# FF1 of two token blocks by seven half-depth products per pair of feature tiles, in a one-core diffusion step

## The chip, the cores and the metric

One core of a Trainium2 chip runs the whole program. The metric is the device time of one execution in microseconds (us). The engines are PE (TensorE, matrix products), DVE (VectorE), ACT (ScalarE), POOL (GpSimd) and SP (SyncE, which issues the DMAs here). Each engine works through its own queue in the order in which the program puts it there; waits between engines go by semaphores.

## What is computed

The kernel is one inference step of a one-layer backbone over 1152 tokens of 1024 features: 1024 latent tokens (chunks 0 to 7 of 128) and 128 context tokens (chunk 8). A state-space mixer and a gated MLP are merged and projected; what concerns the change is the end of the layer:

```python
x = layer_norm(DN_ALPHA * x + gate1 * (merged @ w_out), ln1_g, ln1_b)
h = x * (1.0 + scale2) + shift2
f = jnp.square(jax.nn.relu(h @ w_ff1)) @ w_ff2      # w_ff1 1024 x 4096, w_ff2 4096 x 1024
x = layer_norm(DN_ALPHA * x + gate2 * f, ln2_g, ln2_b)
```

## The kernel before

**Tiling.** Tokens go in three blocks of 384 (`TB`, three chunks of 128 each); blocks 0 and 1 are latent tokens, block 2 holds chunks 6, 7 and the context chunk 8. Every product is made to float32 precision by three passes of the reduced fp32r type: each operand is split into a rounded high part and a remainder (`split`: ACT copies `hi`, another engine subtracts to get `lo`), and `mm3` issues high by high (L89), high by low (L90) and low by high (L91).

**Output projection.** For each block b and each half of the 1024 output features, `tm_half` runs 4 weight tiles over three chunks. `ev_o` evicts: gate (`ot`, DVE), residual with `xr` (DVE), and after the second half the layer norm (`ln_stats` on DVE: per chunk two statistics and a dozen operations on single columns; then a normalization on ACT), a write of the row to `NX` in DRAM, 8 PE transposes per chunk, scale and bias per 128 x 128 square (DVE and ACT in turn), and the split into the activation operands `h2` (ACT and POOL). The residual inputs `xr` come by DMA into four buffers.

**FF1.** Each of 32 feature tiles takes one 128 x 1024 weight tile (`take_fm`, double buffered: raw, high, low) and multiplies it with the three blocks, 24 matmuls of 384 columns each, 72 per tile. `ev_h_of` evicts: relu on ACT, square on DVE, write to `HID` in DRAM. The first two tiles do blocks 0 and 1 first, then block 2.

**FF2.** For each block, 32 steps (`load2`, `split2`): load a weight row tile `w2` and the hidden tile `hraw`, split both (ACT high, DVE low), then 18 matmuls of 512 columns into six banks. `residual` prepares chunk c's final residual: load `NX` into `xa`, multiply by `row_g`, add `row_b`, two DVE operations of 128 x 1024 per chunk, all queued near the start of FF2.

**Order.** The code is written in one order, but the framework sorts each engine's queue by a schedule of its own when it builds the program, within buffers and dependencies. So the first FF2 weights and hidden tiles were loaded and split during FF1, and the weights of the first FF2 steps even during the output projection: their buffers were free.

Of the kernel before, what the change touches and what calls it, by code (L numbers as in the profile page):

```python
# [10 lines left out]
F32 = mybir.dt.float32  # L11
# [24 lines left out]
def tile_trunk(ctx: ExitStack, tc: tile.TileContext, I, O):  # L36
# [43 lines left out]
    def split(raw, hi, lo, eng):  # L80
        A.activation(hi, raw, AF.Copy)  # L81
        if eng is None:
            for e, cs in ((G, slice(0, 512)), (V, slice(512, D))):
                e.tensor_tensor(lo[:, cs], raw[:, cs], hi[:, cs], op=SUB)
        else:
            eng.tensor_tensor(lo, raw, hi, op=SUB)  # L86
# [8 lines left out]
    for n, src in (("xbc", [I["w_xbc"][i] for i in range(12)]),  # L95
                   ("gb", [I["w_gb"][i] for i in range(KT)]), ("ga", [I["w_ga"][i] for i in range(KT)]),
                   ("z", [I["w_z"][i] for i in range(KT)]),
                   ("v", [I["w_v"][i % 8] for i in range(24)]),
                   ("u", [I["w_u"][i] for i in range(KT)]),
                   ("pb", [I["w_proj_b"][i] for i in range(KT)]), ("pa", [I["w_proj_a"][i] for i in range(KT)]),  # L100
                   ("out", [I["w_out"][i % 8] for i in range(24)])):
        wsrc += [(n, s) for s in src]
    wsrc += [("ff1", I["w_ff1"][i]) for i in range(FT)]
    state = {"raw": 0, "split": 0, "use": 0}
    raws, pairs = deque(), deque()
    lo_eng = {"eng": lambda i: G}

    behind, FINE = {}, {0: 4, 1: 2}
# [736 lines left out]
    V.tensor_tensor(S2, modc[1][:, :, 0, :], l1[:, 0, :].unsqueeze(2).broadcast_to([P, KT, 2]), op=MUL)  # L845
    V.tensor_tensor(H2, modc[1][:, :, 0, :], l1[:, 1, :].unsqueeze(2).broadcast_to([P, KT, 2]), op=MUL)
    V.tensor_tensor(H2, H2, modc[1][:, :, 1, :], op=ADD)
    h2 = six("h2")
    for b in range(NB):
        xr = []  # L850

        def load_xr():
            loads = [dma(out=g1[b], in_=GROW[0, b].partition_broadcast(P))] if b < 2 else []
            for c in range(3 * b, 3 * b + 3):
                r = tO.tile([P, D], F32, name="xr", tag="xr", bufs=4)
                loads.append(dma(out=r, in_=XP[c] if c < NL else I["x_prompt"]))
                xr.append(r)
            for ins in loads:
                order(ins, state["last"])

        for half in range(2):
            def ev_o(tt, ps):
                c = 3 * b + tt
                v = 0 if c < NL else 1
                hs = slice(half * 512, (half + 1) * 512)
                t = tO.tile([P, 512], F32, name="ot", tag="ot", bufs=2)
                V.tensor_tensor(t, ps, g1[v][:, hs], op=MUL)
                V.scalar_tensor_tensor(xr[tt][:, hs], xr[tt][:, hs], ALPHA, t, op0=MUL, op1=ADD)
                if half == 0:
                    return  # L870
                r = xr[tt]
                mv = ln_stats([r[:, 0:512], r[:, 512:1024]], tO)
                A.activation(r, r, AF.Identity, bias=mv[:, 2:3], scale=mv[:, 1:2])
                dma(out=NX[c], in_=r)
                for hf in range(2):
                    tp = pxB.tile([P, 4, P], F32, name="h2_ps", tag="aux")
                    ht = tO.tile([P, 4, P], F32, name="h2t", tag="h2t", bufs=2)
                    for a in range(4):
                        k = hf * 4 + a
                        T.transpose(tp[:, a, :], r[:, k * P:(k + 1) * P], ident)  # L880
                    for a in range(4):
                        k = hf * 4 + a
                        if a % 2:
                            A.activation(ht[:, a, :], tp[:, a, :], AF.Identity, bias=H2[:, k, v:v + 1],
                                         scale=S2[:, k, v:v + 1])
                        else:
                            V.tensor_scalar(ht[:, a, :], tp[:, a, :], S2[:, k, v:v + 1], H2[:, k, v:v + 1],
                                            op0=MUL, op1=ADD)
                    split(ht, h2[b][0][:, hf * 4:hf * 4 + 4, tt * P:(tt + 1) * P],
                          h2[b][1][:, hf * 4:hf * 4 + 4, tt * P:(tt + 1) * P], G)  # L890

            tm_half(pmB, "out", mp[b], ev_o, load_xr if half == 0 else None)
# [5 lines left out]
    def ev_h_of(ft):
        def ev_h(b, ps):
            rl = tF.tile([P, 512], F32, name="rl", tag="rl", bufs=2)[:, 0:TB]  # L900
            A.activation(rl, ps, AF.Relu)  # L901
            V.tensor_tensor(rl, rl, rl, op=MUL)  # L902
            dma(out=HID[ft][:, b * TB:(b + 1) * TB], in_=rl)
        return ev_h
# [221 lines left out]
```

## Time and profile before

| | us |
|---|---|
| median of three runs | 1971.39 (1970.22 to 1972.48) |
| profiled execution | 1971.82 |
| its span, first to last instruction | 1970.0 |
| first matmul of FF1 | 1147.48 |
| first matmul of FF2 | 1567.08 |

Times inside the trace count from the start of the span. PE is busy 97% of it; the waits that there are can be read stage by stage. A group of instructions in the page stands as line, engine, operation, output and inputs with shapes, count, then busy time and the mean of one; matmuls overlap their successors, so the step from one start to the next is what one costs, not its duration.

### The profile page before, as it was taken

What the parts mean: (1) busy time and instruction counts of PE and PEld (TensorE: products, weight loads), DVE (VectorE), ACT (ScalarE), POOL (GpSimd) and SP (SyncE); (2) the same over time, 40 slices, a digit from 0 to 9 for tenths busy, and PEclk for the clock granted to TensorE, in tenths of its full rate; (3) what the DMA queues carried; (4) which work ended last, traced back from release to release, by engine and by line L of the source; (5) the groups of instructions that cost most, each with busy time, mean ns of one, the idle gap of its engine ahead of it and who ended that gap; (6) DMA issues with size and microseconds to landing.
All of it is one profiled execution on the core that took longest, in us unless ns stands there. A gap on an engine that the chain in (4) does not pass through costs nothing.

```text
span 1970.0 us, 28049 instructions
## 1 busy us (share of the span) xinstructions
PE 1911.4 (97%) x10747; PEld 1754.1 (89%) x10747; DVE 1110.6 (56%) x2031; ACT 684.2 (35%) x1186; POOL 341.3 (17%) x272
## 2 busy tenths in 40 slices
PE   7999999899999999999999979999999999999998
PEld 4999998788898889999998879999999988888886
DVE  4756857999798353444455873222222474754844
ACT  3443424555413332333332553211111233433431
POOL 0322002333224530254220120000000000000001
PEclk9999999999999999999999989999999999999999
DMA  8144635445575431188445654333223575565540
GB/s 342 58 133 165 209 140 163 129 151 153 194 241 158 121 106 42 33 289 285 140 139 179 203 214 119 107 107 92 91 88 91 184 263 177 168 218 177 182 163 32
DMA packets 139878, 307.58 MB, mean 156 GB/s; under 512 B 14880, under 2 KB 78048, under 8 KB 138592
## 3 DMA queue, kind: packets, MB, share of 16 engines
q1 hardware_dynamic: 139744, 305.80, 47.5%
q8 instruction: 84, 1.38, 0.3%
q14 instruction: 50, 0.41, 0.1%
HBM read 244.23 MB, written 61.51 MB: 155 GB/s over the span
## 4 chain that ended last, share of the span: by engine, by line
PE 82%; DVE 10%; issue 3%; DMA 3%; ACT 1%; POOL 1%; SPq 0%; POOLq 0%; DVEq 0%; ACTq 0%
PE mm_ps L89 19%; PE mm_ps L90 19%; PE mm_ps L91 19%; PE ff_ps L90 6%; PE ff_ps L91 6%; PE ff_ps L89 6%; DVE Fb L581 1%; PE y_ps L601 1%; DVE crow L241 1%; DVE X L662 1%; PE st_ps L523 1%; DVE cbD L584 1%; DVE ssq L670 1%; PE s_ps L734 1%; DVE ada_w L241 1%
## 5 line engine op out<-in xcount | busy, mean ns | idle before, releaser
L89 PE MATMUL mm_ps<-hTh,w_hi 128*128 128x384 f32 x1032 | 355.0, 348 | 0.6 <-ACT gt L620 0.6
L91 PE MATMUL mm_ps<-hTh,w_lo 128*128 128x384 f32 x1032 | 351.0, 340 | 0.0
L90 PE MATMUL mm_ps<-hTl,w_hi 128*128 128x384 f32 x1032 | 351.0, 340 | 0.0
L89 PE MATMUL mm_ps<-h,w_hi 128*128 128x384 f32 x768 | 258.6, 337 | 5.8 <-ACT h L81 5.8
L91 PE MATMUL mm_ps<-h,w_lo 128*128 128x384 f32 x768 | 257.6, 336 | 1.0 <-DVE w_lo L86 1.0
L90 PE MATMUL mm_ps<-h,w_hi 128*128 128x384 f32 x768 | 258.0, 336 | 0.4 <-POOL h L86 0.4
L81 ACT ACTIVATE w_hi<-w_raw 128x1024 fp32r<-128x1024 f32 (+1 forms) x143 | 147.5, 1033 | 277.0 <-PE mm_ps L90 170.3
L90 PE MATMUL ff_ps<-w,hid 128*128 128x512 f32 (+1 forms) x608 | 229.9, 378 | 0.0
L91 PE MATMUL ff_ps<-w,hid 128*128 128x512 f32 (+1 forms) x608 | 229.4, 378 | 0.0
L89 PE MATMUL ff_ps<-w,hid 128*128 128x512 f32 (+1 forms) x608 | 229.4, 378 | 0.0
L86 DVE TENSOR_TENSOR w_lo<-w_raw,w_hi 128x1024 fp32r<-128x1024 f32 (+2 forms) x109 | 135.5, 1245 | 160.9 <-ACT w_hi L81 160.6
L89 PEld LDWEIGHTS mm_ps<-hTh,w_hi 128*128 128x128 f32 x1032 | 195.0, 190 | 10.9 <-issue 7.9
L90 PEld LDWEIGHTS mm_ps<-hTl,w_hi 128*128 128x128 f32 x1032 | 195.1, 189 | 9.5 <-issue 7.0
L91 PEld LDWEIGHTS mm_ps<-hTh,w_lo 128*128 128x128 f32 x1032 | 194.9, 189 | 4.1 <-issue 4.1
L89 PEld LDWEIGHTS mm_ps<-h,w_hi 128*128 128x128 f32 x768 | 145.4, 190 | 6.5 <-ACT h L81 6.5
L902 DVE TENSOR_TENSOR rl<-rl 128x384 f32<-128x384 f32 x96 | 54.2, 565 | 170.4 <-ACT rl L901 170.4
L986 POOL TENSOR_TENSOR xa<-xa,row_lg 128x512 f32<-128x512 f32 (+1 forms) x11 | 15.5, 1421 | 764.9 <-ACT xa L985 638.9
L91 PEld LDWEIGHTS mm_ps<-h,w_lo 128*128 128x128 f32 x768 | 145.2, 189 | 1.3 <-DVE w_lo L86 1.3
L90 PEld LDWEIGHTS mm_ps<-h,w_hi 128*128 128x128 f32 x768 | 145.4, 189 | 0.9 <-POOL h L86 0.9
L86 DVE TENSOR_TENSOR w<-w,w 128x1024 fp32r<-128x1024 f32 x96 | 117.9, 1232 | 47.0 <-PE ff_ps L91 24.3
L89 PEld LDWEIGHTS ff_ps<-w,hid 128*128 128x128 f32 x608 | 114.4, 188 | 21.7
L90 PEld LDWEIGHTS ff_ps<-w,hid 128*128 128x128 f32 x608 | 114.4, 188 | 21.4
(251 smaller groups left out, 3351.9 us busy)
## 6 DMA issues: line engine op xcount, KB each, us to landing
w<-in_w_ff_dram SPq DMA_DIRECT2D x96, 512.0 KB, 5.0
HID<-rl SPq DMA_DIRECT2D x96, 192.0 KB, 2.1
hraw<-HID SPq DMA_DIRECT2D x96, 192.0 KB, 2.4
w_raw<-in_w_ff_dram SPq DMA_DIRECT2D x32, 512.0 KB, 4.0
w_raw<-in_w_v_dram SPq DMA_DIRECT2D x24, 512.0 KB, 3.7
w_raw<-in_w_out_dram SPq DMA_DIRECT2D x24, 512.0 KB, 3.7
Fb<-FB SPq DMA_DIRECT2D x36, 256.0 KB, 4.3
Bb<-FB SPq DMA_DIRECT2D x36, 256.0 KB, 5.0
```

Source lines behind the costliest of these rows:

```text
L81: A.activation(hi, raw, AF.Copy)
L86: eng.tensor_tensor(lo, raw, hi, op=SUB)
L89: T.matmul(ps, s[0], m[0], start=first, stop=False)
L90: T.matmul(ps, s[0], m[1], start=False, stop=False)
L91: return T.matmul(ps, s[1], m[0], start=False, stop=last)
L241: V.scalar_tensor_tensor(wt[:, i, :] if v else junk, wt[:, i, :], 1.0, crow[:, v, :], op0=MUL, op1=MUL, accum_out=outs[:, k, i, v:v + 1])
L523: ins = T.matmul(st, Bk[:, c, g * P:(g + 1) * P], xws[g].rearrange("p h e -> p (h e)"), start=True, stop=True)
L581: V.scalar_tensor_tensor(Fb[:, i, :], Bb[:, i, :], QT[:, c, 3, h:h + 1], Fb[:, i, :], op0=SUB, op1=MIN)
L584: V.scalar_tensor_tensor(cbD[:, i, :], cbL[:, g, :], QT[:, c, 0, h:h + 1], cbD[:, i, :], op0=MUL, op1=ADD)
L601: ins = T.matmul(yp[64 * i:64 * i + 64, q, :], lhs[:, l0 + 64 * j:l0 + 64 * j + 64], rhs[:, j, :], start=n == 0, stop=n == len(terms) - 1)
L662: V.scalar_tensor_tensor(y, xt.rearrange("p (c i) -> p c i", i=P), dskc[:, q:q + 1], y, op0=MUL, op1=ADD)
L902: V.tensor_tensor(rl, rl, rl, op=MUL)
```

## The change

FF1 of blocks 0 and 1 is made as a two by two block product (Strassen's scheme, with Winograd's sums): the two input halves of 512 features by the two token blocks by a pair of feature tiles. Seven products of half depth (12 matmuls each) take the place of eight (96 matmuls); block 2 is still multiplied directly (`direct`, 48 matmuls per pair). That makes 132 matmuls per pair and not 144.

- `combos` builds the activation operands: x11 and x21 after block 0 of the output projection, x22 and the sums q11, q12, q22, q21 with their splits xt4, xt2, xt3, xt1 after block 1. Each covers 128 x 1536.
- `sums` builds four sums of the pair's raw weights (128 x 512 each) and splits them; f0 and f1, the two weight tiles, are split as before.
- The results are combined at eviction: k1 copied by ACT, u2, u3 by DVE, `keep` adds the last term, relu and square in one DVE operation, and writes `HID`. A low half is on DVE everywhere in these stages; POOL has no part in it.
- In the output projection all scale and bias operations are on ACT; `xr` has three buffers and `ot` one; block 2's scale and bias are written in place over `xr`, whose write to `NX` must have landed first. In pair 0 the transposes of chunks 6 to 8 are put behind its half products, and `direct` of block 2 comes last.
- FF2's pool and its first loads come behind all of FF1 in the code.

```diff
+    def operand(name, src):
+        t = blk.tile([P, 2, 4, TB], F32R, name=f"x{name}", tag="blk", bufs=NBLK)
+        split(src, t[:, 0], t[:, 1], V)
+        X[name] = (t[:, 0], t[:, 1])
+
+    def combos(b):
+        q11, q21, q12, q22 = quad[0, 0], quad[1, 0], quad[0, 1], quad[1, 1]
+        if b == 0:
+            operand("11", q11)
+            operand("21", q21)
+            return
+        operand("22", q22)
+        V.tensor_tensor(q11, q12, q11, op=SUB)
+        V.tensor_tensor(q12, q22, q12, op=SUB)
+        V.tensor_tensor(q22, q22, q11, op=SUB)
+        V.tensor_tensor(q21, q22, q21, op=SUB)
+        for name, q in (("t4", q21), ("t2", q22), ("t3", q12), ("t1", q11)):
+            operand(name, q)
...
-                r = tO.tile([P, D], F32, name="xr", tag="xr", bufs=4)
+                r = tO.tile([P, D], F32, name="xr", tag="xr", bufs=3)
...
-                t = tO.tile([P, 512], F32, name="ot", tag="ot", bufs=2)
+                t = tO.tile([P, 512], F32, name="ot", tag="ot", bufs=1)
...
-                    ht = tO.tile([P, 4, P], F32, name="h2t", tag="h2t", bufs=2)
+                    ts = slice(tt * P, (tt + 1) * P)
+                    ht = r.rearrange("p (k f) -> p k f", f=P)[:, 4 * hf:4 * hf + 4, :] if b == 2 else quad[hf, b][:, :, ts]
                     for a in range(4):
                         k = hf * 4 + a
-                        T.transpose(tp[:, a, :], r[:, k * P:(k + 1) * P], ident)
+                        ins = T.transpose(tp[:, a, :], r[:, k * P:(k + 1) * P], ident)
+                        h_first.setdefault((c, hf), ins)
                     for a in range(4):
                         k = hf * 4 + a
-                        if a % 2:
-                            A.activation(ht[:, a, :], tp[:, a, :], AF.Identity, bias=H2[:, k, v:v + 1],
-                                         scale=S2[:, k, v:v + 1])
-                        else:
-                            V.tensor_scalar(ht[:, a, :], tp[:, a, :], S2[:, k, v:v + 1], H2[:, k, v:v + 1],
-                                            op0=MUL, op1=ADD)
-                    split(ht, h2[b][0][:, hf * 4:hf * 4 + 4, tt * P:(tt + 1) * P],
-                          h2[b][1][:, hf * 4:hf * 4 + 4, tt * P:(tt + 1) * P], G)
+                        A.activation(ht[:, a, :], tp[:, a, :], AF.Identity, bias=H2[:, k, v:v + 1],
+                                     scale=S2[:, k, v:v + 1])
+                    if b == 2:
+                        split(ht, h2b[0][:, hf * 4:hf * 4 + 4, ts], h2b[1][:, hf * 4:hf * 4 + 4, ts], V)
 
             tm_half(pmB, "out", mp[b], ev_o, load_xr if half == 0 else None)
+        if b < 2:
+            combos(b)
...
+    NP = FT // 2
+    S_HOME = [blk if p % 2 else blk2 for p in range(NP - 2)] + [blk, blk2]
+    low, high = slice(0, 512), slice(512, D)
+
+    def sums(p):
+        r0, r1 = raw_of.pop(FF0 + 2 * p), raw_of.pop(FF0 + 2 * p + 1)
+        pl = S_HOME[p]
+        t3 = pl.tile([P, 3, 2, 512], F32R, name="S", tag="blk", bufs=NBLK if pl is blk else NBLK2)
+        t4 = (tV if p % 2 else tW).tile([P, 2, 512], F32R, name="S4", tag="S4", bufs=1)
+        ops = [t3[:, 0], t3[:, 1], t3[:, 2], t4]
+        f = [tW.tile([P, 512], F32, name="sum", tag="sum", bufs=2) for i in range(2)]
+        for j, i, x, y, op in ((0, 2, r1[:, low], r1[:, high], ADD), (1, 1, r0[:, low], r1[:, low], SUB),
+                               (0, 0, f[0], r0[:, low], SUB), (0, 3, r0[:, high], f[0], SUB)):
+            V.tensor_tensor(f[j], x, y, op=op)
+            split(f[j], ops[i][:, 0, :], ops[i][:, 1, :], V)
+        return [(t[:, 0, :], t[:, 1, :]) for t in ops]
...
+    def half_product(s, x, cs=slice(0, 512)):
+        ps = pmB.tile([P, TB], F32, name="mm_ps", tag="mm")
+        for k in range(4):
+            ks = slice(cs.start + k * P, cs.start + (k + 1) * P)
+            done = mm3(ps, (s[0][:, ks], s[1][:, ks]), (X[x][0][:, k, :], X[x][1][:, k, :]), k == 0, k == 3)
+        return ps, done
...
+    def keep(p, ft, b, x, y=None, op=ADD):
+        t = (tV if p else tW).tile([P, TB], F32, name="sq", tag="sq", bufs=5 if p else 2)
+        if y is None:
+            A.activation(t, x, AF.Relu)
+            V.tensor_tensor(t, t, t, op=MUL)
+        else:
+            V.tensor_tensor(t, x, y, op=op)
+            V.scalar_tensor_tensor(t, t, 0.0, t, op0=MAX, op1=MUL)
+        dma(out=HID[ft][:, b * TB:(b + 1) * TB], in_=t)
...
+    def next_pair(p, f):
+        if p < NP:
+            nxt.append(take("ff1", 0, 1 - f))
+            if f == 1:
+                S.append(sums(p))
+                more_raw(state["use"] + 1)
+
+    nxt, S = [], deque()
+    next_pair(0, 0)
+    next_pair(0, 1)
+    for p in range(NP):
+        (f0, f1), nxt = nxt, []
+        s2, s3, s1, s4 = S.popleft()
+        ft = 2 * p
+        p1, e1 = half_product(f0, "11")
+        k1, u2, u3 = temp("k1"), temp("u2"), temp("u3")
+        A.activation(k1, p1, AF.Copy)
+        p2, e2 = half_product(f0, "21", high)
+        keep(p, ft, 0, p2, k1)
+        if p:
+            direct(p, ft, f0)
+            next_pair(p + 1, 0)
+        p4, e4 = half_product(f1, "t4", high)
+        if p:
+            direct(p, ft + 1, f1)
+            next_pair(p + 1, 1)
+        p6, e6 = half_product(s2, "t2")
+        V.tensor_tensor(u2, p6, k1, op=ADD)
+        p7, e7 = half_product(s3, "t3")
+        V.tensor_tensor(u3, p7, u2, op=ADD)
+        keep(p, ft + 1, 0, u3, p4, SUB)
+        p5, e5 = half_product(s1, "t1")
+        keep(p, ft + 1, 1, p5, u3)
+        V.tensor_tensor(u2, p5, u2, op=ADD)
+        p3, e3 = half_product(s4, "22")
+        keep(p, ft, 1, p3, u2)
+        if not p:
+            for c, after in ((6, (e4, e6)), (7, (e7, e5)), (8, (e3, e3))):
+                for hf in range(2):
+                    order(h_first[c, hf], after[hf])
+            direct(p, ft, f0)
+            next_pair(p + 1, 0)
+            direct(p, ft + 1, f1)
+            next_pair(p + 1, 1)
+    stV.close()
+    stW.close()
     tF = pool(stB, "tF")
...
-    w0, w1 = take_fm("ff1"), take_fm("ff1", 0)
-    for bs in ((0, 1), (2,)):
-        fm_tile(pmB, w0, h2, ev_h_of(0), bs)
-        fm_tile(pmB, w1, h2, ev_h_of(1), bs)
...
-    for ft in range(2, FT):
-        w = take_fm("ff1")
-        fm_tile(pmB, w, h2, ev_h_of(ft))
```

Three places show what becomes of the order. The first is DVE at the entry to FF1, from the last weight splits of the output projection (`w_lo` of out) on; before, it held residuals (`xr`, `ot`), scale and bias (`h2t`) and splits of FF2's first weights (`w2`):

```order
L868 SCALAR_TENSOR_TENSOR xr_10326<-xr_10326,ot_10530 128x512
L867 TENSOR_TENSOR ot_10579<-mm_ps_10432,g1_0_9580 128x512
L887 TENSOR_SCALAR h2t_10294<-h2_ps_10293,S2_9582,H2_9583 128x128
L887 TENSOR_SCALAR h2t_10306<-h2_ps_10305,S2_9582,H2_9583 128x128
L86 TENSOR_TENSOR w_lo_10682<-w_raw_10510,w_hi_10681 128x1024
```

```order
L86 TENSOR_TENSOR w_lo_10473<-w_raw_10452,w_hi_10472 128x1024
...
L868 TENSOR_TENSOR h2f0_9592<-h2f1_9593,h2f0_9592 128x1536
L940 TENSOR_TENSOR sum_10671<-w_raw_10500 128x512
L940 TENSOR_TENSOR sum_10672<-w_raw_10476,w_raw_10500 128x512
L86 TENSOR_TENSOR w_lo_10497<-w_raw_10476,w_hi_10496 128x1024
...
L869 TENSOR_TENSOR h2f1_9593<-h2f1_9593 128x1536
L86 TENSOR_TENSOR x22_10286<-h2f1_9593,x22_10286 128x1536
...
L870 TENSOR_TENSOR h2f1_9593<-h2f1_9593,h2f0_9592 128x1536
...
L871 TENSOR_TENSOR h2f0_9592<-h2f1_9593,h2f0_9592 128x1536
...
L86 TENSOR_TENSOR xt4_10293<-h2f0_9592,xt4_10293 128x1536
```

The sums of activations (L868 to L871) and the wide splits now stand between the weight splits, w_lo_10497 being that of the first feature tile and xt4 the operand of the third half product. The second place is ACT at the same entry, from the normalization of chunk 6 on (before L873, after L901):

```order
L873 ACTIVATE xr_10326<-xr_10326,ln_mv_10536 128x1024
...
L884 ACTIVATE h2t_10556<-h2_ps_10555,H2_9583,S2_9582 128x128
L884 ACTIVATE h2t_10568<-h2_ps_10567,H2_9583,S2_9582 128x128
...
L81 ACTIVATE h24_9593<-h2t_10556 128x4x128
L81 ACTIVATE h24_9593<-h2t_10568 128x4x128
```

```order
L81 ACTIVATE xt1_10302<-h2f0_9592 128x1536
L901 ACTIVATE xr_10316<-xr_10316,ln_mv_10526 128x1024
...
L913 ACTIVATE xr_10316<-h2_ps_10545,H2_9586,S2_9585 128x128 x4
L81 ACTIVATE h2h_10305<-xr_10316 128x4x128
L81 ACTIVATE S_10669<-sum_10671 128x512
L81 ACTIVATE S_10669<-sum_10672 128x512
L81 ACTIVATE S_10669<-sum_10671 128x512
L81 ACTIVATE S4_10670<-sum_10671 128x512
L81 ACTIVATE S_10869<-sum_10871 128x512
```

The high halves of pair 0's weight sums (S_10669, S4_10670) now stand behind the in-place scale and bias of chunk 6 (L913). The third place is DVE at the passage from FF1 to FF2; before, the splits of hidden tiles (`hid`) of the first nine FF2 steps stood among the evictions of FF1 (`rl`), and at the passage stood

```order
L963 TENSOR_TENSOR xa0_13676<-xa0_13676,row_g_13662 128x1024
L902 TENSOR_TENSOR rl_13645<-rl_13645 128x384
L963 TENSOR_TENSOR xa0_13676<-xa0_13676,row_g_13662 128x1024
L964 TENSOR_TENSOR xa0_13676<-xa0_13676,row_b_13664 128x1024
...
L86 TENSOR_TENSOR hid_13907<-hraw_13876,hid_13907 128x384
```

```order
L960 TENSOR_TENSOR sq_13853<-mm_ps_13840,u2_13699 128x384
L1064 TENSOR_TENSOR xa0_13889<-xa0_13889,row_g_13875 128x1024
L1065 TENSOR_TENSOR xa0_13889<-xa0_13889,row_b_13877 128x1024
L961 SCALAR_TENSOR_TENSOR sq_13853<-sq_13853 128x384
...
L86 TENSOR_TENSOR w2_14117<-w2_14087,w2_14117 128x1024
...
L1064 TENSOR_TENSOR xa2_13891<-xa2_13891,row_g_13875 128x1024 x3
L1065 TENSOR_TENSOR xa2_13891<-xa2_13891,row_b_13877 128x1024
L86 TENSOR_TENSOR hid_13872<-hraw_13864,hid_13872 128x384
```

sq_13853 is the last `keep` of FF1, which reads the last half product; hid_13872 is the first hidden tile of FF2. Between the two now stand 18 operations of 128 x 1024 (15 of `residual`, 3 splits of `w2`).

## Rows read from the trace of the kernel before

**Rows 1.** The page, part 1: busy time of each engine, share of the span, instructions
```profile
PE 1911.4 (97%) x10747; PEld 1754.1 (89%) x10747; DVE 1110.6 (56%) x2031; ACT 684.2 (35%) x1186; POOL 341.3 (17%) x272
```

**Rows 2.** The page, part 5: costliest groups, one pass of FF1's three; squares
```profile
L89 PE MATMUL mm_ps<-h,w_hi 128*128 128x384 f32 x768 | 258.6, 337 | 5.8 <-ACT h L81 5.8
...
L902 DVE TENSOR_TENSOR rl<-rl 128x384 f32<-128x384 f32 x96 | 54.2, 565 | 170.4 <-ACT rl L901 170.4
```

**Rows 3.** Timeline of PE, 1147 to 1569 us: start, duration, line, idle before
```profile
1147.48 0.42 PE L89 MATMUL mm_ps<-h,w_hi 128*128 128x384 f32 x1
...
1150.06 0.33 PE L90 MATMUL mm_ps<-h,w_hi 128*128 128x384 f32 x1
...
1151.97 0.33 PE L89 MATMUL mm_ps<-h,w_hi 128*128 128x384 f32 x1
...
1156.44 1.01 PE L89 MATMUL mm_ps<-h,w_hi 128*128 128x384 f32 x2 [3.27 <-ACT h L81]
1157.25 0.52 PE L90 MATMUL mm_ps<-h,w_hi 128*128 128x384 f32 x1
...
1161.41 0.52 PE L91 MATMUL mm_ps<-h,w_lo 128*128 128x384 f32 x1
...
1567.08 0.39 PE L89 MATMUL ff_ps<-w,hid 128*128 128x512 f32 x1
```

**Rows 4.** PE's waits from 1140 to 1200 us: total, times, longest
```profile
PE mm_ps L89 <- ACT h L81: 5.8, 2, 3.3
PE h_ps L880 <- ACT h2t L884: 3.7, 3, 3.1
```

**Rows 5.** Windows: length, busy time of each engine, granted clock, DMA share, GB/s
```profile
1080.00:1147.00 67.00, 67.00 (x317) 55.44 (x316) 57.30 (x153) 38.42 (x55) 13.78 (x10) 1.00 0.69 247
1147.00:1164.00 17.00, 12.74 (x60) 12.10 (x59) 17.00 (x29) 8.78 (x12) 3.74 (x3) 0.80 0.51 186
1164.00:1200.00 36.00, 29.44 (x160) 27.53 (x159) 15.60 (x56) 18.05 (x32) 7.48 (x6) 0.86 0.36 119
1200.00:1550.00 350.00, 350.00 (x2021) 350.00 (x2020) 82.58 (x119) 71.49 (x119) 0.00 (x0) 1.00 0.32 97
```

**Rows 6.** Lines of DVE, 1060 to 1200 us, by form: busy, mean ns
```profile
L867 DVE TENSOR_TENSOR ot<-mm_ps,g 128x512 f32<-128x512 f32 x17 | 11.4, 681 | 2.4 <-PE mm_ps L91 2.2
```

**Rows 7.** Lines of ACT, 1060 to 1200 us, by form
```profile
L884 ACT ACTIVATE h2t<-h_ps,H,S 128x128 f32<-128x128 f32 x36 | 15.6, 455 | 18.6 <-DVE h2t L887 18.6
L81 ACT ACTIVATE h<-h2t 128x512 fp32r<-128x512 f32 x18 | 10.9, 627 | 0.2
```

**Rows 8.** Timeline of DVE: a layer norm's small operations, then the passage
```profile
1120.81 0.14 DVE L197 TENSOR_SCALAR ln_mv<-ln_mv 128x1 f32<-128x1 f32 x1
...
1125.22 0.16 DVE L210 SCALAR_TENSOR_TENSOR ln_mv<-ln_mv 128x1 f32<-128x1 f32 x1
...
1569.37 1.22 DVE L963 TENSOR_TENSOR xa<-xa,row_g 128x1024 f32<-128x1024 f32 x1
...
1582.37 1.22 DVE L86 TENSOR_TENSOR w<-w,w 128x1024 fp32r<-128x1024 f32 x1
1583.50 1.22 DVE L963 TENSOR_TENSOR xa<-xa,row_g 128x1024 f32<-128x1024 f32 x1
...
1597.40 1.22 DVE L964 TENSOR_TENSOR xa<-xa,row_b 128x1024 f32<-128x1024 f32 x1
```

**Rows 9.** The page, part 6: DMA issues, KB each, us to landing
```profile
hraw<-HID SPq DMA_DIRECT2D x96, 192.0 KB, 2.4
w_raw<-in_w_ff_dram SPq DMA_DIRECT2D x32, 512.0 KB, 4.0
```

**Rows 10.** DMA issues from 1040 to 1200 us
```profile
NX<-xr SPq DMA_DIRECT2D x9, 512.0 KB, 4.5
...
xr<-XP SPq DMA_DIRECT2D x8, 512.0 KB, 6.0
```

**Rows 11.** DMA from 1140 to 1147 us, when the engines are full
```profile
DMA packets 769, 2.79 MB, mean 399 GB/s; under 512 B 91, under 2 KB 91, under 8 KB 768
```

More of the change, by code (lines that the diff above doesn't have):

```diff
@@ L102, in tile_trunk @@
         wsrc += [(n, s) for s in src]
+    FF0 = len(wsrc)
     wsrc += [("ff1", I["w_ff1"][i]) for i in range(FT)]
     state = {"raw": 0, "split": 0, "use": 0}
-    raws, pairs = deque(), deque()
+    raws, pairs, raw_of = deque(), deque(), {}
     lo_eng = {"eng": lambda i: G}
@@ L142, in more_split @@
             pairs.append((hi, lo))
+            raw_of[i] = raw
             state["split"] += 1
@@ L836, in tile_trunk @@
     lo_eng["eng"] = lambda i: V
+    stW = ExitStack()
+    tW = pool(stW, "tW")
     stO = ExitStack()
@@ L847, in tile_trunk @@
     V.tensor_tensor(H2, H2, modc[1][:, :, 1, :], op=ADD)
-    h2 = six("h2")
+    h2f = [blk2.tile([P, KT, TB], F32, name=f"h2f{b}", tag="blk", bufs=NBLK2) for b in range(2)]
+    quad = {(r, b): h2f[b][:, 4 * r:4 * r + 4, :] for r in range(2) for b in range(2)}
+    X, h_first = {}, {}
+    def operand(name, src):
[15 more added lines that the diff above has]
+            operand(name, q)
     for b in range(NB):
+        if b == 2:
+            h2b = [blk2.tile([P, KT, TB], F32R, name=f"h2{n}", tag="blk", bufs=NBLK2) for n in ("h", "l")]
         xr = []
@@ L892, in tile_trunk @@
+                    if b == 2:
+                        split(ht, h2b[0][:, hf * 4:hf * 4 + 4, ts], h2b[1][:, hf * 4:hf * 4 + 4, ts], V)
             tm_half(pmB, "out", mp[b], ev_o, load_xr if half == 0 else None)
+        if b < 2:
+            combos(b)
     stO.close()
-    tF = pool(stB, "tF")
[L898 to L904, printed above, removed]
@@ L906, in tile_trunk @@
-    w0, w1 = take_fm("ff1"), take_fm("ff1", 0)
-    for bs in ((0, 1), (2,)):
-        fm_tile(pmB, w0, h2, ev_h_of(0), bs)
-        fm_tile(pmB, w1, h2, ev_h_of(1), bs)
+    stV = ExitStack()
+    tV = pool(stV, "tV")
+    NP = FT // 2
[13 more added lines that the diff above has]
+        return [(t[:, 0, :], t[:, 1, :]) for t in ops]
@@ new lines, in half_product, with temp @@
+    def half_product(s, x, cs=slice(0, 512)):
[4 more added lines that the diff above has]
+        return ps, done
+    def temp(name):
+        return tW.tile([P, TB], F32, name=name, tag=name, bufs=1)
+    def keep(p, ft, b, x, y=None, op=ADD):
[7 more added lines that the diff above has]
+        dma(out=HID[ft][:, b * TB:(b + 1) * TB], in_=t)
@@ new lines, in direct @@
+    def direct(p, ft, w):
+        fm_block(pmB, [x.rearrange("p (k f) -> p k f", f=P) for x in w], [None, None, h2b], 2,
+                 lambda b, ps: keep(p, ft, b, ps))
+    def next_pair(p, f):
[41 more added lines that the diff above has]
+            next_pair(p + 1, 1)
```

## The prediction

> **What bounds the kernel now.** The page's first part comes first: PE is busy 97% of the span [rows 1]. What matters is where it isn't, so I read windows of the stages around the change next [rows 5]: in the output projection (1080 to 1147 us) PE works without a gap, in the body of FF1 (1200 to 1550) too, with DVE at 24%; at the entry to FF1 (1147 to 1200) it works 42 of 53 us, and at the lower clock for part of that. The waits there are ACT's and DVE's: activations of chunks 5 to 8 still on their way through layer norm, scale and split [rows 4]. At the passage to FF2 PE's first FF2 matmul follows FF1 without a wait [rows 3], while DVE works off the residuals until 1598 us [rows 8]: that backlog is hidden, since the first hidden tiles had been split long before.
>
> One matmul of 384 columns costs (1151.97 - 1150.06) / 11 = 0.1736 us at full clock; after the idle of 3.27 us it cost (1161.41 - 1157.25) / 13 = 0.32 [rows 3]. FF1 lasted 1567.08 - 1147.48 = 419.6 us; its 3 x 768 = 2304 matmuls [rows 2] account for 400.0. So 19.6 us were lost at the entry (waits, slow clock, the last 24 transposes).
>
> **What is removed.** 12 matmuls of 144 in each of 16 pairs: 192 x 0.1736 = **-33.3 us**, all on the path, since PE is the bound in the body. The Trainium skill, page "TensorE: Matmul & The Clock Gate", section on the 56 ns gap, gives a matmul N columns at 2.4 GHz plus about 2.5 ns, 162.5 ns here; by it the gain would be 31.2 us. The row's 173.6 ns is this kernel's own, and decides.
>
> **The body of FF1.** A pair now takes 132 x 0.1736 = 22.9 us on PE. DVE's part of it: eight operations of 512 (four sums, four low halves) at 0.68 [rows 6], two weight splits of 1024 at 1.22 [rows 8], and thirteen of 384 at 0.565 [rows 2], together 15.2 us. ACT has some 6 us. Both fit, six banks let PE run ahead, and POOL no longer works beside DVE: nothing, at most 0.5 us per pair (8 us) if a weight load holds up DVE's queue. I take 0.
>
> **The output projection.** DVE gets x11 and x21 (1536 wide; 512 costs 0.68, 1024 costs 1.22 with a step of 1.13 [rows 6, 8], so by extension some 1.66 each) and loses half the scale and bias operations. With three buffers a load of `xr` waits until the chunk three before has been transposed and written; it takes 6.0 us to land [rows 10]. The residual (`xr`) operations stand in DVE's queue ahead of weight splits, and PE waits for those. PE waits for nothing there now [rows 5]; walking the queue I find the splits between in time and 4 us late. **+2** (0 to 4).
>
> **The entry.** I follow the queues from 1147.5, where the output projection ends.
> 1. The first half product needs w_lo of the first tile, which stands behind two sums that need the second tile's raw weights; its buffer frees only after the residual of chunk 7, whose load waits for chunk 4's transposes (about 1137). Load 6.0, operation and split 1.9, raw load 4.0 [rows 9], sums and split 2.4: w_lo at about 1151.
> 2. xt4, operand of the third half product: behind w_lo stand q12, x22, q22 and q21, then xt4 itself, five of 1.66, one weight split and some eight of 0.6, 14 us: about 1165. PE has made two half products (4.2) by 1155 and waits ten.
> 3. Chunk 6: three more wide splits (5.0), the rest of the statistics (about 3), and some 40 small operations; before, three chunks' worth took 1120.81 to 1125.3, one weight split included, so 3.3 [rows 8]. Normalization about 1177. Its write to `NX` takes 4.5 to land [rows 10], and only then may scale and bias overwrite it in place: 1182. Behind these on ACT stand the weight sums' high halves: four scales at a step near 0.36 and four copies of 0.63 [rows 7], with DVE's low halves and sums between, so the fourth half product starts at about 1186.
> 4. Four half products (8.3) on a slow start (before, 16 matmuls at 0.32, +2.4) end at about 1197. Meanwhile ACT must wait for sums of pair 1, whose raw load is issued only when pair 0's sums are made (1187 + 4.0), and then does 20 scales and five splits (10 us): block 2's operands are complete at about 1203. Its 48 matmuls and another slow start end at **1214**.
>
> Without any loss pair 0 would end at 1147.5 + 22.9; so 43.6 us are lost instead of 19.6: **+24**. The bounds: if the chain of step 3 is 13 us shorter (the write lands in 2.4 like a smaller transfer, and the small operations hide), +11; if loads are late at each of the three waits, +30.
>
> **The passage to FF2.** Let E be the end of the last half product. DVE can't make the last `keep` earlier, and between it and the first hidden tile's low half stand 18 operations of 1024, whose step is 1.13 [rows 8]: 0.6 + 20.3 + 0.6 + 0.6 = E + 22. The third pass of the first FF2 step needs it. The first two passes, 12 matmuls, can go before, as soon as the hidden tile is loaded: that load stands on SP behind 17 loads of 512 KB, at 399 GB/s [rows 11] 1.31 us each, from about E - 10: E + 15. So PE loses 22 less 12 x 0.23 = 19.2 us, plus some 3 for two slow starts. **+22** (18 to 26). Before: nothing. FF2 itself and the tail are unchanged.
>
> **The sum.** Against the profiled execution's 1971.8 (0.4 above the median): -33.3 + 2 + 24 + 22 = +14.7, 1986.5 us, so **1986** against the median. With all low ends -33.3 + 0 + 11 + 18 = -4.3, 1967.5; with all high ends +34.7, 2006.5.
>
> **Rivals.**
> - *The passage is hidden* (faster, 1964). If loads of `NX` and the new weights land so early that DVE has its 18 operations done by E, the +22 falls to nothing. It decides by where DVE stands at E: each operation done before saves 1.13, and 13 of 18 make the change even. For it: DVE has 7.7 us per pair free. Against it: the queue puts 18 behind an instruction that can't run before E, so they can't move, whatever the loads do. It needs the queue not to be worked in order. 0.08.
> - *The entry is short* (1968 to 1975). The chain of step 3 overlaps better than I walked it, and both gains and stalls cancel: the +24 becomes +11 or less, with the passage at its low end. 0.12.
> - *The body stalls as well* (1995 to 2010). Each pair's sums stand ahead of the evictions on DVE and need raw weights whose buffer was freed only by the sums before. If that wait is longer than PE's six banks cover, say 0.5 to 1.5 us per pair, 8 to 24 us come on top. Against it: two weight loads of 4.0 us per 22.9 us. 0.14.
> - That the change doesn't do what it says is out: the matmuls are counted in the queue.
>
> **How the numbers follow.** The forecast (slower, 1986, its own range 1976 to 1997) gets 0.66. The measurement tells changes over about 0.2%, 4 us, from none: faster means below 1967.5, slower above 1975.3. The passage rival is faster; half of the short entry is the same, a quarter each faster and slower; the forecast's lower shoulder adds a little to the same: faster 0.11, same 0.08, slower 0.81. The range leaves out 0.2: below 1968 (0.11) and above 2003 (0.09).
>
> **What would show it.** In the profile after: the body of FF1 with PE without gaps and pairs 22.9 us apart (right or wrong on the -33.3); PE's waits between 1147 and 1215 of some 35 us, named xt4's split on ACT and DVE and S's high half on ACT, with the chunk's `NX` write in front; the first FF2 matmul some 15 us behind the last half product and its third pass at E + 22, waiting for `hid` on DVE while DVE runs `xa` operations one upon the other. If the first FF2 matmuls follow within 5 us, the passage step is wrong; if pair 0 ends before 1200, the entry step is.

## The result, and the profile after

The changed kernel takes 1986.5 us (median of 4 runs, 1985.8 to 1988.4) against 1971.3 (1970.2 to 1972.5): a ratio of 1.0079, interval 1.0061 to 1.0096. It is slower, by 15 us where 14.7 were forecast. The profiled execution took 1988.4, its span 1986.6.

The page, parts 1 and 5, answers to [rows 1, 2]: PE has 192 instructions less, DVE 221 more, and a wait that was not there before, for the first hidden tile of FF2, has become the largest on PE's matmuls.

```profile
PE 1883.0 (95%) x10555; PEld 1724.3 (87%) x10555; DVE 1243.9 (63%) x2252; ACT 714.6 (36%) x1233; POOL 316.2 (16%) x254
...
L89 PE MATMUL ff_ps<-w,hid 128*128 128x512 f32 (+1 forms) x608 | 230.8, 380 | 19.7 <-ACT hid L81 19.7
```

Windows of the stages (length, busy time of PE, PEld, DVE, ACT, POOL, granted clock, DMA share, GB/s), which answer to [rows 5]; the last is new and covers the passage:

```profile
1080.00:1150.00 70.00, 67.33 (x313) 55.27 (x312) 46.24 (x126) 41.82 (x72) 0.00 (x0) 0.98 0.59 190
1150.00:1220.00 70.00, 39.79 (x178) 36.69 (x178) 48.84 (x100) 31.18 (x53) 0.00 (x0) 0.73 0.19 65
1220.00:1550.00 330.00, 330.00 (x1906) 330.00 (x1905) 201.58 (x331) 88.56 (x134) 0.00 (x0) 1.00 0.36 111
1550.00:1600.00 50.00, 28.76 (x132) 24.83 (x131) 42.89 (x52) 15.73 (x22) 0.00 (x0) 0.80 0.82 296
```

Read from top to bottom: a small gap in the output projection, 30 us of idle PE in the 70 us of the entry, a body without a gap, and 21 us of idle PE at the passage. In both gaps the mean granted clock is below 1 (0.73 and 0.80): some of the matmuls beside them run at the lower of the clock's two levels.

Where PE waits, in its timeline (start, duration, line, idle before and its releaser), which answers to [rows 3, 4]. The first row is FF1's first matmul, the row of 1216.98 is the first of pair 1, that of 1560.00 FF1's last:

```profile
1118.22 0.50 PE L90 MATMUL mm_ps<-w_lo,mh 128*128 128x512 f32 x1 [2.67 <-DVE w_lo L86]
...
1150.72 0.33 PE L89 MATMUL mm_ps<-x,w_hi 128*128 128x384 f32 x1
...
1153.60 0.55 PE L91 MATMUL mm_ps<-x,w_lo 128*128 128x384 f32 x1 [2.01 <-DVE w_lo L86]
...
1165.66 0.69 PE L89 MATMUL mm_ps<-xt,w_hi 128*128 128x384 f32 x1 [6.72 <-ACT xt L81]
1168.38 0.69 PE L90 MATMUL mm_ps<-xt,w_hi 128*128 128x384 f32 x1 [2.04 <-DVE xt L86]
...
1179.64 1.11 PE L909 MATMUL h_ps<-ident,xr 128*128 128x128 f32 x4 [7.37 <-ACT xr L901]
...
1187.71 0.69 PE L89 MATMUL mm_ps<-xt,S 128*128 128x384 f32 x1 [6.96 <-ACT S L81]
...
1205.72 1.01 PE L89 MATMUL mm_ps<-h2h,w_hi 128*128 128x384 f32 x2 [3.17 <-ACT h2h L81]
...
1216.98 0.33 PE L89 MATMUL mm_ps<-x,w_hi 128*128 128x384 f32 x1
...
1560.00 0.34 PE L91 MATMUL mm_ps<-x,S 128*128 128x384 f32 x1
...
1580.08 0.79 PE L89 MATMUL ff_ps<-w,hid 128*128 128x512 f32 x1 [19.74 <-ACT hid L81]
...
1586.35 1.64 PE L91 MATMUL ff_ps<-w,hid 128*128 128x512 f32 x6 [1.50 <-DVE hid L86]
```

The account from these rows. Body: pairs 1 to 15 took (1560.17 - 1216.98) / 15 = 22.88 us each, so 12 matmuls a pair are saved in full and nothing is given back. Entry: pair 0 lasted 1216.98 - 1150.72 = 66.3 us, 43.4 more than the 22.88 of a pair, where 19.6 were lost before: +23.8. Passage: idle 19.74 + 1.50, and the twelve matmuls between took about 1.9 more than at full clock (a step of 0.43 in place of 0.23 for eight of them): +23.1. Output projection: +2.7. Sum: -33.3 + 23.8 + 23.1 + 2.7 = +16.3; the two profiled executions differ by 16.6.

FF1's first matmul comes at 1146.4 to 1153.7 us in the profiled executions below, and much of that spread is there from one run to the next: e1 and e2, whose code up to the end of FF1 is that of the changed kernel, have it at 1153.7 and 1147.7, the changed kernel at 1150.7. So places are told from it (**R**) or, at the passage, from the end of FF1's last matmul (**E**). Each experiment is given as a ratio to repeats of the kernel before that ran beside it; a difference of two ratios is given in us of 1970, and its interval is 3 to 6 us to either side.

### The profile page after: what moved, and what is told of

Read it like the earlier page. It is cut to its first block, busy times and chain, and to the rows that moved or that the text cites. A ratio compares the mean times of both kernels' runs of the same rounds, so it can differ in the third digit from the quotient of the medians.

```text
span 1986.6 us, 27903 instructions
## 1 busy us (share of the span) xinstructions
PE 1883.0 (95%) x10555; PEld 1724.3 (87%) x10555; DVE 1243.9 (63%) x2252; ACT 714.6 (36%) x1233; POOL 316.2 (16%) x254
## 4 chain that ended last, share of the span: by engine, by line
PE 76%; DVE 12%; DMA 5%; issue 3%; ACT 2%; POOL 1%; SPq 1%; POOLq 0%; DVEq 0%; ACTq 0%
PE mm_ps L89 18%; PE mm_ps L90 18%; PE mm_ps L91 17%; PE ff_ps L91 6%; PE ff_ps L89 6%; PE ff_ps L90 6%; DVE Fb L583 1%; DVE crow L243 1%; DVE cbD L586 1%; PE y_ps L603 1%; DVE w_lo L86 1%; DVE X L664 1%; PE s_ps L736 1%; PE st_ps L525 1%; DVE ssq L672 1%
## 5 line engine op out<-in xcount | busy, mean ns | idle before, releaser
L89 PE MATMUL ff_ps<-w,hid 128*128 128x512 f32 (+1 forms) x608 | 230.8, 380 | 19.7 <-ACT hid L81 19.7
L86 DVE TENSOR_TENSOR w_lo<-w_raw,w_hi 128x1024 fp32r<-128x1024 f32 (+2 forms) x109 | 131.1, 1205 | 165.7 <-ACT w_hi L81 165.0
L89 PEld LDWEIGHTS ff_ps<-w,hid 128*128 128x128 f32 x608 | 115.0, 189 | 41.6 <-ACT hid L81 20.1
L91 PEld LDWEIGHTS ff_ps<-w,hid 128*128 128x128 f32 x608 | 114.1, 188 | 23.3 <-DVE hid L86 1.9
L90 PEld LDWEIGHTS ff_ps<-w,hid 128*128 128x128 f32 x608 | 115.0, 189 | 21.7
L81 ACT ACTIVATE hid<-hraw 128x384 fp32r<-128x384 f32 x96 | 50.1, 524 | 208.6 <-PE ff_ps L91 185.5
L86 DVE TENSOR_TENSOR hid<-hraw,hid 128x384 fp32r<-128x384 f32 x96 | 53.1, 555 | 112.8 <-ACT hid L81 112.7
L81 ACT ACTIVATE w<-w 128x1024 fp32r<-128x1024 f32 x96 | 98.6, 1049 | 43.4 <-DMA w<-in_w_ff_dram 38.0
L86 POOL TENSOR_TENSOR w_lo<-w_raw,w_hi 128x1024 fp32r<-128x1024 f32 x34 | 84.2, 2477 | 91.8 <-ACT w_hi L81 91.8
L89 PE MATMUL mm_ps<-h2h,w_hi 128*128 128x384 f32 x256 | 86.8, 340 | 3.2 <-ACT h2h L81 3.2
L90 PE MATMUL mm_ps<-h2l,w_hi 128*128 128x384 f32 x256 | 86.7, 339 | 0.0
```

The costliest lines, as they stand in the source:

```text
L89: T.matmul(ps, s[0], m[0], start=first, stop=False)
L90: T.matmul(ps, s[0], m[1], start=False, stop=False)
L91: return T.matmul(ps, s[1], m[0], start=False, stop=last)
```

## The experiments

The question after the result is not whether the 33 us were saved, but what holds the two gaps open that swallow them: how much work there is, or in which order each in-order queue does it.

### The residual work behind the hidden tiles: e1_res_late

```diff
     def residual(c):
         t = xa[c // 3][:, c % 3, :]
-        dma(out=t, in_=NX[c])
-        V.tensor_tensor(t, t, rows["g"], op=MUL)
-        V.tensor_tensor(t, t, rows["b"], op=ADD)
+        order(dma(out=t, in_=NX[c]), hraw_dma[2 + 2 * c])
+        order(V.tensor_tensor(t, t, rows["g"], op=MUL), hid_lo[2 + 2 * c])
+        order(V.tensor_tensor(t, t, rows["b"], op=ADD), hid_lo[2 + 2 * c])
```

> The nine residual tiles of FF2 (their loads of NX and the two VectorE passes over each) are ordered behind hidden tiles 2, 4, 6 and so on of FF2, loads and passes both; FF1 is untouched. Theory: of the 26 us between the last FF1 matmul and the third pass of FF2 in the changed kernel, most is in-order queueing, the hidden tile's load behind about 5 MB of other loads (19.7 us) and its low half behind 18 residual passes on VectorE (26 us). With both moved back the third pass should come 6 to 10 us after the last FF1 matmul, so 15 to 18 us less than the changed kernel's 1986.5: about 1970. Rival: the passage is the round trip of HID through memory (write, load, split), which moving the residual work doesn't shorten: then at most 5 us less, 1982 or more.

Measured: ratio to the kernel before 1.0021 (1.0010 to 1.0033), so 11.4 us less than the changed kernel. The timeline of PE at the passage:

```profile
1562.31 0.34 PE L91 MATMUL mm_ps<-x,S 128*128 128x384 f32 x1
...
1570.69 0.80 PE L89 MATMUL ff_ps<-w,hid 128*128 128x512 f32 x1 [8.04 <-ACT hid L81]
...
1575.86 1.54 PE L91 MATMUL ff_ps<-w,hid 128*128 128x512 f32 x6
```

Half of the passage was order and no work: the wait is 8.0 in place of 19.7 + 1.5. The gain is less than expected (the third pass comes at E + 13.4, not at E + 6 to 10), since a wait of 8 us remains, and the twelve matmuls after it again run at 0.43, which costs 2.4. SP's queue shows what remains (start, duration, line, transfers):

```profile
1564.40 1.85 SPq L962 DMA_DIRECT2D HID<-sq  x3
1566.34 2.30 SPq L1034 DMA_DIRECT2D hraw<-HID  x4
```

The hidden tile of step 0 was written some 400 us earlier (the first write of `HID` goes out at 1165.0), yet its load is issued behind the last three writes of FF1.

### Only the passes on VectorE moved: e2_res_ops_late

As e1, but with the load left where it was:

```diff
-        order(dma(out=t, in_=NX[c]), hraw_dma[2 + 2 * c])
+        dma(out=t, in_=NX[c])
```

> Only the VectorE passes over the residual tiles are ordered behind the hidden tiles' low halves; their loads stay where the changed kernel has them. Theory of two limits close together: the hidden tile still lands behind the other loads, so FF2's first matmul stays at 18 to 20 us after FF1's last and the third pass follows within 2 us of it: about 5 us less than the changed kernel, 1981 to 1983. Rival, VectorE's backlog alone sets the passage: 15 us or more less, 1971. Rival, transfers alone: nothing, 1986.5.

Measured: ratio 1.0098 (1.0076 to 1.0120), against 1.0079 for the changed kernel. Nothing is gained. PE at the passage, then SP:

```profile
1556.32 0.34 PE L91 MATMUL mm_ps<-x,S 128*128 128x384 f32 x1
...
1579.11 0.79 PE L89 MATMUL ff_ps<-w,hid 128*128 128x512 f32 x1 [22.45 <-ACT hid L81]
...
1583.81 1.55 PE L91 MATMUL ff_ps<-w,hid 128*128 128x512 f32 x6
```

```profile
1559.84 2.87 SPq L1064 DMA_DIRECT2D xa<-NX  x3
1563.73 2.88 SPq L962 DMA_DIRECT2D HID<-sq  x3
1571.21 1.31 SPq L1032 DMA_DIRECT2D w<-in_w_ff_dram  x3
1572.62 19.65 SPq L1034 DMA_DIRECT2D hraw<-HID  x14
```

The third pass no longer waits for VectorE, but it starts at E + 27.3, where the changed kernel's started at E + 26.2: in this kernel the load alone holds the passage. That is the third of the three answers named, and not the one I held. VectorE is done with FF1's last square at 1559.3, but SP, which issues every transfer, stands with the loads of `NX` and the weights, so the last writes of `HID` go out at 1563.7 and the hidden tiles' loads at 1572.6.

The load did not stay where it was, though. With the passes moved, the framework sorted SP's queue anew and put three weight loads (1571.21) ahead of the hidden tiles', which in the changed kernel come behind them (rows of 1572.56 and 1581.32 further down). These weight loads wait for VectorE's splits of earlier weights, and so the hidden tile's load goes out at E + 16.1 where it went out at E + 12.4. So e2 shows that moving the passes alone gains nothing, but not what their removal would give with the load left in its place, nor what the loads moved alone would give, which was not run.

### Two hidden tiles before FF1 ends: e6_hid_early

The edit of e1, and FF2's helpers put ahead of FF1's loop; in the last pair two hidden tiles go to the memory that block 2's activations leave:

```diff
+        if p == NP - 1:
+            early[0] = blk2.tile([P, 8, TB], F32R, name="he", tag="blk", bufs=NBLK2)
+            for i in range(2):
+                load2(i + 1)
+                split2()
...
-    load2(1)
-    load2(2)
-    split2()
+    load2(3)
+    load2(4)
     split2()
```

> The residual work is late as in e1_res_late, and the first two hidden tiles of FF2 are read back into a tile of the pool that block 2's activations leave after their last product in FF1, instead of into memory that the FF1 temporaries hold until the last write of HID has landed; with them the first two weight tiles are loaded and split before FF1 ends. Theory: the 8.0 us that e1_res_late still waits is the queue position of the hidden tile's load, behind the three last writes of HID, since its memory is theirs; with two tiles ready FF2 starts within 1 us of FF1's last matmul, steps 0 and 1 cover some 8 us, and the third tile is there by then: 8 to 10 us less than e1_res_late, about 1961 to 1964, that is 0.995 to 0.997 of the kernel before. Rival: FF2's third step waits instead (its tile still stands behind the last writes, loads and splits), and only half of the 8 us comes back: 1968.

Measured: ratio 0.9970 (0.9960 to 0.9980), 10 us less than e1 and now faster than the kernel before. PE's waits from 1530 to 1640 us (total, times, longest), and the timeline there:

```profile
PE ff_ps L89 <- ACT hid L81: 0.8, 1, 0.8
PE ff_ps L89 <- ACT he L81: 0.2, 1, 0.2
```

```profile
1554.89 0.34 PE L91 MATMUL mm_ps<-x,S 128*128 128x384 f32 x1
1555.44 0.50 PE L89 MATMUL ff_ps<-w,he 128*128 128x512 f32 x1 [0.21 <-ACT he L81]
1555.77 0.39 PE L90 MATMUL ff_ps<-w,he 128*128 128x512 f32 x1
1556.00 0.39 PE L89 MATMUL ff_ps<-w,he 128*128 128x512 f32 x1
```

The loss at the passage is down from 23 to 1 us, and the rival's wait in the third step is 0.8 us. Without a long idle stretch ahead of it FF2 runs at full clock (steps of 0.23, granted clock 1.00), so the slow start of the changed kernel was a follow-up of the wait. What is shown is that the place of the first loads behind the last writes of `HID` cost some 10 us. Why they had that place is read from the code: the changed kernel gives them the memory of FF1's temporaries, which those writes read. e6 changes the memory and the place in the code together, so the runs do not separate the two; and in the changed kernel the load is issued 1.3 us after the last write, before any of the three has landed (7.8 to 9.4 us after their issue), so its issue did not wait for their landing.

### The entry without the combinations: e4_no_combos

```diff
         operand("22", q22)
-        V.tensor_tensor(q11, q12, q11, op=SUB)
-        V.tensor_tensor(q12, q22, q12, op=SUB)
-        V.tensor_tensor(q22, q22, q11, op=SUB)
-        V.tensor_tensor(q21, q22, q21, op=SUB)
-        for name, q in (("t4", q21), ("t2", q22), ("t3", q12), ("t1", q11)):
-            operand(name, q)
+        for name in ("t4", "t2", "t3", "t1"):
+            X[name] = X["11"]
```

> Leaves out the four activation combinations and their splits (the four 1536-wide subtractions and four low halves on VectorE, four high halves on ScalarE); the products that would read them read the split of the first quarter instead, so FF1's values are not those of the reference and only the time of the rest is looked at. Theory: the combinations hold the path for the wait for t4 (6.7 and 2.0 us) and push the norm of chunks 6 to 8 back by about 13 us of VectorE work, of which the transposes, the sums of pair 0 and block 2's products all follow: pair 0 ends 10 to 14 us sooner, 1973 to 1977. Rival: the entry is set by the raw weight loads of pair 0's and pair 1's sums: under 5 us less, 1982 or more.

Measured: ratio 1.0018 (1.0006 to 1.0030), 12.0 us less than the changed kernel. Pair 1 starts at R + 53.1 (R is 1148.08), where it was R + 66.3. PE:

```profile
1148.08 0.33 PE L89 MATMUL mm_ps<-x,w_hi 128*128 128x384 f32 x1
...
1165.12 1.11 PE L905 MATMUL h_ps<-ident,xr 128*128 128x128 f32 x4 [7.71 <-ACT xr L897]
...
1173.19 0.69 PE L89 MATMUL mm_ps<-x,S 128*128 128x384 f32 x1 [6.95 <-ACT S L81]
...
1191.14 1.01 PE L89 MATMUL mm_ps<-h2h,w_hi 128*128 128x384 f32 x2 [3.17 <-ACT h2h L81]
```

The combinations account for half of the entry's extra loss, and the rest of the chain simply moves forward: the waits for the norm, for S and for h2h are as long as before (7.7, 7.0, 3.2). The rival, raw weight loads, is out as the main cause: it named less than 5 us.

### The weight sums ahead of the norm: e3_sums_first

```diff
-    S_HOME = [blk if p % 2 else blk2 for p in range(NP - 2)] + [blk, blk2]
+    S_HOME = [blk if p % 2 or not p else blk2 for p in range(NP - 2)] + [blk, blk2]
...
-            V.tensor_tensor(f[j], x, y, op=op)
-            split(f[j], ops[i][:, 0, :], ops[i][:, 1, :], V)
+            first = V.tensor_tensor(f[j], x, y, op=op)
+            if p == 1 and i == 2:
+                order(first, ln_end[-1])
+            last = split(f[j], ops[i][:, 0, :], ops[i][:, 1, :], V)
+        if p == 0:
+            for ins in ln_iter[-3:]:
+                order(ins, last)
```

(`ln_iter` and `ln_end` hold the first shift and the last operation of each layer norm.)

> Entry only: the weight sums of pair 0 stand ahead of the rest of the layer norm of chunks 6 to 8 on VectorE and ScalarE, their tile lies in the other pool, and the sums of pair 1 stand behind that layer norm; no work is added or taken away. Theory: pair 0's products with sums wait at 1187.7 for ScalarE's high half, which is queued behind the norm, its transposes' eviction and the split of h2, and block 2's products wait at 1205.7 because evictions of transposes stand behind sums of pair 1 on ScalarE; with the order changed the products with sums begin at 1176 to 1179, block 2's at 1197 to 1201, and pair 0 ends 6 to 9 us sooner: 1978 to 1981. Rival: the entry is bound by the amount of VectorE and ScalarE work ahead of block 2's products, and the norm, now 5 us later, gives back what the sums gain: 1985 to 1988.

Measured: ratio 1.0058 (1.0040 to 1.0075), 4.1 us less than the changed kernel and between the two answers. The two intervals overlap, so the time alone would not show a gain; the trace does: pair 0 lasts 61.2 us in place of 66.3. PE, then ACT (R is 1148.98):

```profile
1176.14 0.69 PE L89 MATMUL mm_ps<-xt,S 128*128 128x384 f32 x1 [6.10 <-ACT S L81]
...
1198.97 1.01 PE L89 MATMUL mm_ps<-h2h,w_hi 128*128 128x384 f32 x2 [3.23 <-ACT h2h L81]
```

```profile
1181.84 3.52 ACT L903 ACTIVATE xr<-xr,ln_mv 128x1024 f32<-128x1024 f32 x3 [3.57 <-DVE ln_mv L214]
```

The products with sums start at R + 27.2 in place of R + 37.0, ten us sooner, but the norm comes at R + 32.9 in place of R + 27.6, and block 2's products at R + 50.0 in place of R + 55.0. Half of the gain is given back to the norm. So this order (pair 0's sums ahead of the norm and pair 1's behind it, which e3 does not separate) is worth some 5 us. That no swap of the two can give more, since both stand ahead of block 2's products on VectorE and ScalarE, is argued and not shown.

### Both: e7_both

The edits of e3 and e6 in one kernel.

> e3_sums_first and e6_hid_early in one kernel. Theory: entry and passage are 340 us apart and have no engine's backlog in common, so the gains add: 4 us less than e6_hid_early, about 1957 to 1960, 0.993 to 0.995 of the kernel before. Rival: the earlier end of pair 0 only meets the body's VectorE or transfers sooner, and nothing is added: the time of e6_hid_early.

Measured: ratio 0.9947 (0.9932 to 0.9962): 4.5 us less than e6, where e3 gave 4.1 alone. In the trace pair 0 lasts 60.4 us in place of e6's 65.5, and PE waits 0.9 us at the passage. Entry and passage add up.

### Pair 0 without Strassen: e8_pair0_direct

If the loss of the entry is the chain ahead of the first combined products, it can be covered by products that need none. The edit of e6, and:

```diff
+        if not p:
+            S.popleft()
+            e = [full(0, i, f, b) for i, f in ((0, f0), (1, f1)) for b in range(2)]
...
+            direct(0, 0, f0)
+            next_pair(1, 0)
+            direct(0, 1, f1)
+            next_pair(1, 1)
+            continue
```

(`full` multiplies a block by both halves, 24 matmuls; the combinations, unchanged, are ordered behind block 2's split; h2l moves to the other pool.)

> As e6_hid_early, and pair 0 of FF1 gives up Strassen: its two blocks are done by 96 whole products (12 matmuls more than the seven half products), from the splits of the four quarters, so that neither weight sums nor combinations stand ahead of them; the combinations are ordered behind the split of block 2 and are first read in pair 1. Theory: the entry's loss is the chain of VectorE and ScalarE work ahead of pair 0's first combined product and ahead of block 2, not the amount of TensorE work; 16.7 us of products that are ready at once cover the layer norm of chunks 6 to 8, block 2's products start some 30 us after the output projection's last matmul instead of 55, and for 2.1 us more matmuls pair 0 ends 23 to 28 us sooner: 1936 to 1942, 0.983 to 0.986 of the kernel before. Rival: the combinations, moved into pair 1, then hold up pair 1 (13 us of VectorE work between block 2's split and the product with t4) and half comes back: 1950.

Measured: ratio 0.9877 (0.9856 to 0.9898), median 1947.4, 24 us faster than the kernel before. PE's timeline, then the window of the entry:

```profile
1184.04 1.01 PE L89 MATMUL mm_ps<-h2h,w_hi 128*128 128x384 f32 x2 [3.23 <-ACT h2h L81]
...
1194.72 0.33 PE L89 MATMUL mm_ps<-x,w_hi 128*128 128x384 f32 x1
...
1204.15 0.45 PE L91 MATMUL mm_ps<-xt,w_lo 128*128 128x384 f32 x1 [0.25 <-DVE w_lo L86]
```

```profile
1150.00:1220.00 70.00, 60.02 (x321) 56.75 (x320) 54.60 (x106) 37.31 (x64) 0.00 (x0) 0.90 0.28 100
```

R is 1152.1, so pair 1 starts at R + 42.6 in place of e6's R + 65.5: 22.9 us sooner, at the lower end of the 23 to 28 expected, with block 2 at R + 32 (some 30 expected). The kernel gained 18.3 against e6, not 22.9. From R to the end of the span the two profiled executions differ by 19.1 us, which agrees: 22.9 less in pair 0, 0.6 more in the fifteen pairs behind it, and 3.2 more in FF2, where PE waits 2.9 us for a hidden tile and then runs at the lower clock for a while, and where e6 waited 1.0. The rival (pair 1 held up by the combinations) is out: from the start of pair 1 to 1520 us PE has one gap, the 0.25 us of a weight split at t4's product in the row of 1204.15.

## Why the prediction was right, step by step

- **The saving** (-33.3): right. A pair takes 22.88 us against 22.9 forecast. The step is 22.88 / 132 = 0.1733 us, that of [rows 3]. The Trainium skill's page "TensorE: Matmul & The Clock Gate", section "Wait — 56ns, not 53.3ns?", gives N columns at 2.4 GHz plus about 2.5 ns, from which 162.5 ns is an estimate for 384 columns. The trace does not agree with it: by that estimate a pair would have taken 21.5 us.
- **The body** (0): right, 330.00 of 330.00 us busy. DVE worked 201.6 us in them, 14.0 us a pair where 15.2 were counted. One reason given carried nothing: POOL did no work in the body before either (0.00 in [rows 5]).
- **The output projection** (+2): 2.67, the one wait in its place, behind x11 and x21 on DVE.
- **The entry** (+24): +23.8, and by its own steps, told from FF1's first matmul (1147.5 in the prediction, 1150.7 in the trace): first w_lo +3.5 forecast, +2.9 measured; t4's low half +17.5 and +17.7; norm +29.5 and +27.6; the fourth half product +38.5 and +37.0; block 2 +55.5 and +55.0; end +66.5 and +66.3. One term in it was mis-sized: the write to `NX` was put at 4.5 us [rows 10] ahead of the overwriting; here it landed 2.7 us after its issue, and ACT, which had the norm of chunks 7 and 8 to do meanwhile, idled for it only 0.44. The experiments bear the mechanism out: e4, e3 and e8 move the end of pair 0 by changing what stands ahead of its products. Row of ACT:

```profile
1182.29 1.51 ACT L913 ACTIVATE xr<-h_ps,H,S 128x128 f32<-128x128 f32 x4 [0.44 <-DMA NX<-xr]
```

- **The passage** (+22): +23.1, but in part by luck. The step put the hidden tile's load at E + 15 and the end of DVE's backlog of 18 operations at E + 22, and so took the backlog for the bound. In the trace the third pass does wait last for DVE, whose low half comes at 1585.75 behind `xa` operations one upon the other, but both came some 4 us later than forecast. The last `keep`, put right behind E, reads its product at E + 4.1 (1564.25), and so the backlog ends late; the load arrived at E + 19.3 (1579.5). So the two end close together, and the backlog costs PE only the last 1.5 us. The sum came out near all the same because 3 us for slow starts were added to it: with a backlog that ends at E + 22 the first twelve matmuls would have been done before, even at 0.43 each, and their slow start would have cost nothing. What I missed is that the load stands on SP behind the last writes of `HID`, whose memory it takes by the code, and those behind the loads of `NX`. In the changed kernel, SP, ACT and DVE:

```profile
1564.83 2.88 SPq L1063 DMA_DIRECT2D xa<-NX  x3
1568.72 2.88 SPq L962 DMA_DIRECT2D HID<-sq  x3
1572.56 4.09 SPq L1034 DMA_DIRECT2D hraw<-HID  x4
1581.32 2.08 SPq L1032 DMA_DIRECT2D w<-in_w_ff_dram  x3
```

```profile
1579.51 2.12 ACT L81 ACTIVATE hid<-hraw 128x384 fp32r<-128x384 f32 x4 [4.59 <-DMA hraw<-HID]
```

```profile
1564.25 0.55 DVE L960 TENSOR_TENSOR sq<-mm_ps,u 128x384 f32<-128x384 f32 x1
...
1585.75 1.02 DVE L86 TENSOR_TENSOR hid<-hraw,hid 128x384 fp32r<-128x384 f32 x2
```

  The forecast of 17 loads from E - 10 fits the time of issue (E + 12.3 forecast, E + 12.4 measured); the load itself then took 6.9 us in place of the median 2.4 of [rows 9], with the DMA engines full. Had I believed the backlog and moved only it, I would have gained nothing, as e2 did.
- **The rivals** did not come: the passage was not hidden, the entry not short, the body did not stall.

No engine's total of work was the limit, but how much of it stood ahead of the first product that needed it: e8 makes 12 matmuls more on PE than e6 and 14 of some 2250 operations less on DVE (8 us of its busy time), in another order, and is 18 us faster.

## What to carry to other kernels

A scheme that saves matmuls by preparing operands saved time here only where the preparation lay under other matmuls; the first tile after a change of stage has nothing above it, so do that tile in the plain way and start the scheme with the next. When two queues end close together at a gap, move each alone to find which of them binds, and look in the trace whether the move left the other queue as it was. And the first loads of a stage can stand in their queue behind the last writes of the stage before, though their data were ready long ago: give them an early place, and memory that is free by then.

## What the runs showed of the hardware that I had not expected

Behind PE's idle stretches of 2.01, 6.96, 3.17 and 19.74 us (rows of 1153.60, 1187.71, 1205.72 and 1580.08 above) matmuls ran at the lower clock, with a granted clock of 0.50 to 0.53: the step was 0.32 for 384 columns and 0.43 for 512 in place of 0.17 and 0.23. Behind the 1.50 us of 1586.35 they did not (1.00), nor in e6, where FF2's first matmuls ran at 0.23. The wait at the passage cost some 2 us beyond its length (1.9 in the changed kernel, 2.4 in e1). The DMA engines moved 408 to 430 GB/s for a stretch of the passage, more than the 399 of [rows 11]; slices of the changed kernel from 1545 to 1590 us (forty, GB/s):

```profile
GB/s 328 379 397 302 333 290 200 346 408 411 331 353 371 361 413 423 408 430 419 419 411 411 411 408 408 415 385 401 395 280 83 19 15 135 328 233 284 337 306 191
```
